# Output stage of a hybrid decoder step: conditioning loads issued by GpSimd, and the order of two small products in the SSD part

## The chip, the cores and the metric

One core of one Trainium2 chip. The metric is the device time of one execution in microseconds (us); several runs give a median. Weights come from HBM in the course of the kernel, so both TensorE and the 16 DMA engines matter.

## The reference

One layer of a decoder works on 288 tokens at once: 256 of a prompt and 8 x 4 of samples, with width 2048, in float32.

```python
mod = silu(c) @ w_ada + b_ada                      # 6 parts: sh1, sc1, g1, sh2, sc2, g2
h = rmsnorm(x, norm1) * (1 + sc1) + sh1
u_pool, z, xbc, dt_raw = split(h @ w_in)
pool_out = pool_mixer(u_pool)                      # trailing means, a linear map per group
ssd_out = ssd_mixer(z, conv(xbc), dt_raw)          # below
x = x + g1 * (concat(pool_out, ssd_out) @ w_out)   # the output stage
h2 = rmsnorm(x, norm2) * (1 + sc2) + sh2
x = x + g2 * conv_ffn(h2)                          # gate and val, conv of gate, w_down
y = rmsnorm(x, norm_f)
```

The SSD mixer has 24 heads of 64 in 4 groups. In a chunk, y = (C B^T * decay) x dt is summed with what the state at the chunk's start gives, then comes D x, a gate and a norm. For the samples that second part is one product with the state handed in, `yo` in the kernel.

## The kernel before, in words

All token matrices lie as channels x tokens: 16 tiles of 128 channels (k) by 288 tokens. A projection takes for each output tile m the weight in two halves of 128 x 1024 float32 (512 KB, `raw_out_3_0` is the first half of output tile 3). A half is loaded by `load` (L279, one DMA), cast by ScalarE to its high part `whi` (L298), and VectorE subtracts to get the low part `wlo` (L300). TensorE then makes three products for each k (`mm3`, L312 to L314): whi with the high operand, whi with the low one, wlo with the high one.

Buffers of `raw` come from rings. In the output stage 8 are used for weights (`raw`), and others for the conditioning (`rawa`); `whi` and `wlo` have 4 each. A load waits until its buffer was read for the last time, and what is queued behind it on the issuing engine waits too.

The conditioning (`mod` of the reference) is computed beside the other work. `ada_visits` (L421) loads pieces of w_ada (512 KB each, `raw_adap_4_6_1`: part 4, k=6, half 1) and multiplies them with silu(c) in `whole` (L414), 32 products of 128 x 512 in a *visit*. In the output stage, part 4 has four visits of 4 k's, so 8 loads each; the visits stand on TensorE behind the output tiles m=3, 6, 9 and 12. All loads are issued by SyncE (SP, L279).

In the SSD part, `ssd_group` runs for four groups g beside the projections, in steps cut by `yield`. The main loop pulls one step between stretches of a projection, so that ScalarE and VectorE make an operand while TensorE does something else. One step made the transposes of B (L794 to L796), the next the product C B^T (L799 to L805) and two DMAs to `sbx`. `outputs` (L864) forms for each t in 0, 1, 2 (two heads) an output in one PSUM tile: the sample columns NP:N sum the product of `yo` (L868) and two of `xdt` with the decays `e` (L872); the other columns are for the prompt.

In the output stage, `out_units(m)` (L1131) makes tile m in two accumulators: `mm_out` for the SSD operands, which VectorE then scales (`oz`, L1179), and `mm_outp` for the pool operands. `residual` (L1168) adds both to x: VectorE makes the prompt's part (L1169) and `rs` (L1172), POOL adds rs to x (L1175). `squares` squares the finished tile on ScalarE (`sqa`, L1185) and POOL adds it to `rt` (L1189). x itself is loaded by SyncE four tiles at a time (L1213). Later parts of the program are allocated and begun when their buffers allow: POOL's load of `stf` (L1280) and two copies into `gb` (L1292) are of the FFN stage, but a scheduler places them in the output stage.

The order of instructions on each engine is decided by a scheduler when the program is built: each engine has one fixed list and works through it in order. A change of which engine issues a load changes the lists of several engines.

Of the kernel before, what the change touches and what calls it, by code (L numbers as in the profile page):

```python
# [18 lines left out]
P = 128  # L19
D = 2048  # L20
KT = D // P
NP = 256
NB, NL = 8, 4
NS = NB * NL
N = NP + NS
# [29 lines left out]
AK, AO = 2, 4  # L55
# [28 lines left out]
def _xbc_chunks(bi):  # L84
    (k0, gk), (a, b) = BLOCKS[bi]
    mper = RAWC // (gk * P)
    cuts = [a, *([4, 8] if bi == 0 else []), *range(a + (12 if bi == 0 else mper), b, mper), b]
    return [(list(range(k0, k0 + gk)), list(range(m, n))) for m, n in zip(cuts, cuts[1:])]
# [35 lines left out]
def _halves(nk):  # L124
    return [(0, 8), (8, nk - 8)]
# [41 lines left out]
def kernel(ctx: ExitStack, tc, ins, outs):  # L167
    nc = tc.nc
    S = _STREAM
    wflat = ins["wflat"]  # L170
# [11 lines left out]
    def aux(name):  # L182
        return px.tile([P, 512], F32, tag="aux", name=name)
# [10 lines left out]
    seli = vec[:, K_SEL:K_SEL + 32]  # L194
# [78 lines left out]

    wp = [None]

    def load(key, ring="raw"):
        off, cols = S.items[key]
        t = wp[0].tile([P, RAWC], F32, tag=ring, name="raw_" + "_".join(map(str, key)))
        nc.sync.dma_start(t[:, :cols], wflat[off:off + P * cols].rearrange("(p n) -> p n", p=P))  # L279
        return t  # L280

    queue = deque(_need_order())
    ahead = {}
    nloads = [0]

    def top_up():

        while queue and nloads[0] - min((n for n, _ in ahead.values()), default=nloads[0]) < RAW0 + RAW1 + RAWA:
            key = queue.popleft()
            ahead[key] = (nloads[0], load(key))  # L290
            nloads[0] += 1
# [4 lines left out]
    def split_steps(raw, a, n, name):  # L296
        hi = wp[0].tile([P, RAWC], F32R, tag="whi", name="whi_" + name)
        yield nc.scalar.copy(hi[:, :n], raw[:, a:a + n])  # L298
        lo = wp[0].tile([P, RAWC], F32R, tag="wlo", name="wlo_" + name)
        yield hi, lo, nc.vector.tensor_tensor(lo[:, :n], raw[:, a:a + n], hi[:, :n].bitcast(F32), ALU.subtract)  # L300
# [37 lines left out]
    def ada_sb(ps, nb, name, r=P):  # L338
        asb = kp.tile([P, 512], F32, tag="asb", name="asb_" + name)
        nc.scalar.copy(asb[0:r, :nb], ps[0:r, :nb])  # L340
        return asb
# [66 lines left out]
    def whole(ps, chunks, step, pin, begun=0):  # L408

        n = 0  # L410
        for k, h, raw in chunks[::-1]:
            for j in (2 * h, 2 * h + 1):
                with tc.high_priority() if n else nullcontext():
                    i = nc.tensor.matmul(ps[32 * j:32 * j + 32, :], sc_c[:, k, :],  # L414
                                         raw[:, 512 * (j % 2):512 * (j % 2) + 512], start=not begun and k == step - 1,
                                         stop=k == KT - step, tile_position=(0, 32 * j))
                if n or pin:
                    tc.keep_in_program_order(i)
                n += 1

    def ada_visits(parts, step, ps=None, begun=0, apart=False):  # L421

        plan = [(part, k0) for part in parts for k0 in range(begun, KT, step)]
        ahead, end = [], None

        def chunks(v):
            part, k0 = plan[v]
            for k in range(k0, k0 + step):
                for h in range(2):
                    ahead.append((k, h, load(("adap", part, k, h), "rawa")))  # L430
                    if apart:
                        yield
            for _ in range(1 if apart else 3):
                yield

        yield from chunks(0)
        for v, (part, k0) in enumerate(plan):
            if end:
                ada_end(*end)
                end = None  # L440
            if k0 == 0:
                ps = pa.tile([P, 512], F32, tag="ada", name=f"adap{part}")
            whole(ps, ahead, step, True, begun)
            ahead.clear()
            if k0 + step == KT:
                end = part, ada_sb(ps, 512, f"p{part}")
            yield
            if v + 1 < len(plan):
                yield from chunks(v + 1)
        ada_end(*end)  # L450
        yield

    def ada_end(part, asb):
        pt = ada_tr(asb, 512, f"p{part}")
        with tc.high_priority():
            nc.vector.tensor_tensor(ada[:, part].rearrange("p (j i) c -> p i j c", j=4),
                                    pt.rearrange("p (i j c) -> p i j c", i=4, j=4)[:, :, :, 0:NC9],
                                    bada[:, part].rearrange("p (j i) -> p i j", j=4).unsqueeze(3)
                                    .to_broadcast([P, 4, 4, NC9]), ALU.add)
        if part == 4:  # L460
            ada_scale(1, 4, vec[:, V_N2:V_N2 + KT], 0, KT)
# [76 lines left out]
    for q in range(4):  # L538
        t = mx.tile([P, 4, N], F32, tag="blk", name=f"xa{q}", bufs=4)
# [232 lines left out]
    def ssd_group(g):  # L772
# [10 lines left out]
        xdt = kp.tile([P, 3, G6], F32, tag="hmod", name=f"xdt{g}", bufs=2)  # L783
# [10 lines left out]
        for c in range(3):  # L794
            nc.tensor.transpose(pt[:, c * P:(c + 1) * P], toks(3, c), ident)
        nc.scalar.copy(bt.rearrange("p c n -> p (c n)"), pt[:, 0:3 * P])  # L796

        yield
        pcb = aux(f"cb{g}")  # L799
        for c in range(3):  # L800
            n = min(P, N - c * P)
# [5 lines left out]
        q = slice(NS * g, NS * g + NS)  # L807
        nc.gpsimd.dma_start(sbx[q, 0:P], bt[0:NS, 2, :])
        nc.gpsimd.dma_start(sbx[q, P:P + G6], xde[0:NS, 2, :])
        yield  # L810

        s1 = sx[0].tile([P, G6], F32, tag="s1", name=f"s1_{g}")
# [24 lines left out]
        yo = sx[0].tile([P, G6], F32, tag="yo", name=f"yo{g}")  # L837
# [26 lines left out]
        def outputs(t, e, ec):  # L864
            assert (g, t) in zdone
            pq = aux(f"y{g}_{t}")
            rows = [slice(0, 64), slice(64, P)]
            nc.tensor.matmul(pq[:, NP:N], yo[:, P * t:P * t + P], seli, start=True, stop=False)  # L868
            for i, r in enumerate(rows):
                f = slice(64 * (2 * t + i), 64 * (2 * t + i) + 64)  # L870
                f = slice(64 * (2 * t + i), 64 * (2 * t + i) + 64)
                nc.tensor.matmul(pq[r, NP:N], xdt[:, 2, f], e[:, i, NP:N], start=False, stop=True)  # L872
            for i, r in enumerate(rows):
                f = slice(64 * (2 * t + i), 64 * (2 * t + i) + 64)
                nc.tensor.matmul(pq[r, 0:P], xdt[:, 0, f], e[:, i, 0:P], start=True, stop=True)
            for i, r in enumerate(rows):
                f = slice(64 * (2 * t + i), 64 * (2 * t + i) + 64)
                nc.tensor.matmul(pq[r, P:NP], xdt[:, 1, f], e[:, i, P:NP], start=True, stop=False)
                nc.tensor.matmul(pq[r, P:NP], s1[:, f], ec[:, i, :], start=False, stop=True)
            yt = cf[:, t, 0:N]  # L880
            nc.vector.scalar_tensor_tensor(out=yt, in0=yt,
                                           scalar=vec[:, V_D + 3 * g + t:V_D + 3 * g + t + 1],
                                           in1=pq[:, :N], op0=ALU.mult, op1=ALU.add)
            zt = zy[g][:, t, :]
            nc.vector.tensor_tensor(zt, zt, yt, ALU.mult)
            sq = kp.tile([P, N], F32, tag="xsq", name=f"ysq{g}_{t}", bufs=2)
            nc.scalar.activation(sq, zt, AF.Square)
            if g + t == 0:
                nc.gpsimd.tensor_copy(ssq, sq)
            else:  # L890
                nc.gpsimd.tensor_tensor(ssq, ssq, sq, ALU.add)
# [9 lines left out]
        outputs(1, *dec[1])  # L901
        yield
        outputs(2, *dec[2])
        yield

# [54 lines left out]
    adas = ada_visits((2, 3), AK)  # L960
    with in_order(*(e.engine for e in (nc.tensor, nc.scalar, nc.vector))):
# [3 lines left out]
        for q in range(4):  # L965
# [5 lines left out]
            for i in range(4):  # L971
                nc.tensor.matmul(ssum[32 * i:32 * i + 32, :N], ones[:, 0:32], sq[:, i, :],
                                 start=(q == 0), stop=(q == 3), tile_position=(0, 32 * i))
# [16 lines left out]
        parts = [split_steps(t, 0, len(ms) * P, f"xbc0_{i}") for i, (t, (_, ms)) in  # L990
                 enumerate(zip(first, _xbc_chunks(0)))]
# [36 lines left out]
    def take(gn, n):  # L1028
        for _ in range(n):
            next(gn)  # L1030
            yield

    ssd3 = ssd_group(3)
    back = chain(conv0, h0s(0), zip2(ssd_group(0), conv_group(1)), h0s(1),
                 zip2(ssd_group(1), conv_group(2)), h0s(2), zip2(ssd_group(2), conv_group(3)), h0s(3),
                 zip2(take(ssd3, TK), chain(pool_units(UEARLY[0]), pool_units(UEARLY[1]))))
    credit = {}
# [9 lines left out]
    for bi in range(len(BLOCKS)):  # L1047
        last = bi + 1 == len(BLOCKS)
        top_up()
        if last:  # L1050
# [6 lines left out]
            raw = load(("dt",))[:, :KT * NH].rearrange("p (k h) -> p k h", h=NH)  # L1057
# [6 lines left out]
            ps = pm.tile([P, 512], F32, tag="mm", name="mm_dt")  # L1064
# [26 lines left out]
    n = 0  # L1091
# [13 lines left out]
            next(late[m])  # L1105
    drain(adas)
    wp[0].move("rawa", "rawa", "raw")
    adas = ada_visits((4,), AO, apart=True)
    for h, (_, n) in enumerate(_halves(KT)):
        ready[("out", 0, h)] = split(load(("out", 0, h)), 0, n * P, f"out_0_{h}")  # L1110
    drain(back)
# [11 lines left out]
    for g in range(4):  # L1123
        for t in range(3):
            k = 4 + 3 * g + t
# [273 lines left out]
    with in_order(nc.sync.engine, nc.scalar.engine, nc.vector.engine):  # L1399
        for i, (m0, n, own) in enumerate(YC):  # L1400
            v = x[:, m0:m0 + n, :]
            eng, r = (nc.gpsimd, rstdf) if own else (nc.vector, rstdp)
# [148 lines left out]
```

## Time and profile before

| | us |
|---|---|
| median of 3 runs | 1345.59 (1345.21 to 1346.12) |
| profiled execution | 1346.4 |
| its span | 1344.6 |
| TensorE busy in the span | 1328.4 |
| VectorE, ScalarE, GpSimd busy | 822.8, 580.3, 223.1 |
| SSD groups in the span (about) | 250 to 362 |
| output stage in the span | 361.4 to 488 |

The profile is a trace of one execution. Its page gives each engine's busy time, the DMA queues, the waits and the costliest groups of instructions; other views show a timeline of one engine, the busy time in chosen windows, or one tile. In a row, `PE` is TensorE, `PEld` its weight loads, `DVE` VectorE, `ACT` ScalarE, `POOL` GpSimd, and `SP` or `SPq` SyncE and its queue of DMA issues. `out<-in` names the tiles. Brackets at a row's end give the idle time of the engine ahead of the instruction and what released it. There are two queues for the DMAs of the program: q1 (hardware_dynamic) carries 310.72 MB that SyncE and ScalarE issue, q0 (software_dynamic) 9.69 MB that POOL issues.

### The profile page before, as it was taken

To read this page: it belongs to the slowest core of one execution; us is meant where nothing else is said; L and a number is where in the kernel's file an instruction comes from. 1 tells how busy PE (TensorE), PEld (TensorE's weight loads), DVE (VectorE), ACT (ScalarE), POOL (GpSimd) and SP (SyncE) were. 2 spreads that over 40 slices of the span, in tenths; PEclk is the share of its full clock that TensorE was granted. 3 is DMA by queue.
4 is the path that set the end of the run, shared out by engine and by line. 5 is a ranking of instruction groups with operands and counts; after the bars stand their busy time and mean duration, and the time that the engine had idled before them with its cause. 6 is when DMAs were issued, how large, how long until landed. Compare 5 with 4: busy or idle time off the path is not lost.

```text
span 1344.6 us, 26157 instructions
## 1 busy us (share of the span) xinstructions
PE 1328.4 (99%) x10523; PEld 1247.1 (93%) x10523; DVE 822.8 (61%) x1375; ACT 580.3 (43%) x913; POOL 223.1 (17%) x449
## 2 busy tenths in 40 slices
PE   9999999999999999999999999999999999999997
PEld 7899988776788889999999999999999999999997
DVE  5776569878754568555565455665655556666543
ACT  5243244677733335433433333434433334443552
POOL 0000012123122222102121001221210011122221
PEclk9999999999999999999999999999999999999999
DMA  9999778888898866687455455555544555555521
GB/s 375 405 370 373 272 266 308 308 318 299 306 402 354 324 237 228 229 311 282 172 201 171 167 179 184 203 185 196 182 162 172 190 190 193 194 190 191 188 69 71
DMA packets 97482, 323.19 MB, mean 240 GB/s; under 512 B 10768, under 2 KB 19920, under 8 KB 97360
## 3 DMA queue, kind: packets, MB, share of 16 engines
q1 hardware_dynamic: 93456, 310.72, 63.0%
q0 software_dynamic: 3184, 9.69, 2.0%
q8 instruction: 82, 1.34, 0.4%
q10 hardware_dynamic: 720, 1.11, 0.2%
q14 instruction: 40, 0.33, 0.1%
HBM read 309.78 MB, written 10.39 MB: 238 GB/s over the span
## 4 chain that ended last, share of the span: by engine, by line
PE 93%; DMA 3%; DVE 2%; ACT 1%; issue 0%; POOL 0%; SPq 0%; DVEq 0%; ACTq 0%; POOLq 0%
PE mm_down L313 7%; PE mm_down L312 7%; PE mm_down L314 7%; PE mm_val L313 6%; PE mm_gate L313 6%; PE mm_gate L312 6%; PE mm_gate L314 6%; PE mm_val L314 6%; PE mm_val L312 6%; PE xbc L312 4%; PE xbc L313 4%; PE xbc L314 4%; PE adap L414 4%; PE adag L381 2%; DMA raw_adap<-wflat 2%; PE mm_out L314 2%
## 5 line engine op out<-in xcount | busy, mean ns | idle before, releaser
L313 PE MATMUL mm_down<-al,whi_down 128*128 128x288 f32 x688 | 202.5, 294 | 0.0
L312 PE MATMUL mm_down<-ah,whi_down 128*128 128x288 f32 x688 | 202.4, 294 | 0.0
L314 PE MATMUL mm_down<-ah,wlo_down 128*128 128x288 f32 x688 | 202.0, 294 | 0.0
L313 PE MATMUL mm_val<-h2l,whi_val 128*128 128x288 f32 x640 | 189.1, 296 | 0.0
L313 PE MATMUL mm_gate<-h2l,whi_gate 128*128 128x288 f32 x640 | 189.1, 295 | 0.0
L314 PE MATMUL mm_val<-h2h,wlo_val 128*128 128x288 f32 x640 | 188.4, 294 | 0.0
L314 PE MATMUL mm_gate<-h2h,wlo_gate 128*128 128x288 f32 x640 | 188.4, 294 | 0.0
L312 PE MATMUL mm_gate<-h2h,whi_gate 128*128 128x288 f32 x640 | 188.3, 294 | 0.0
L312 PE MATMUL mm_val<-h2h,whi_val 128*128 128x288 f32 x640 | 188.0, 294 | 0.0
L300 DVE TENSOR_TENSOR wlo_down<-raw_down,whi_down 128x1024 fp32r<-128x1024 f32 x96 | 109.1, 1137 | 115.4 <-ACT whi_down L298 115.4
L300 DVE TENSOR_TENSOR wlo_gate<-raw_gate,whi_gate 128x1024 fp32r<-128x1024 f32 x80 | 98.9, 1237 | 131.5 <-ACT whi_gate L298 131.5
L298 ACT CAST whi_down<-raw_down 128x1024 fp32r<-128x1024 f32 x96 | 92.3, 962 | 164.7 <-PE mm_down L313 135.3
L298 ACT CAST whi_gate<-raw_gate 128x1024 fp32r<-128x1024 f32 x80 | 84.1, 1051 | 156.6 <-PE mm_gate L313 80.3
L298 ACT CAST whi_val<-raw_val 128x1024 fp32r<-128x1024 f32 x80 | 84.1, 1052 | 129.3 <-issue 110.1
L312 PE MATMUL xbc<-h1h,whi_xbc 128*128 128x288 f32 x448 | 133.1, 300 | 0.8 <-ACT h1h L491 0.7
L313 PE MATMUL xbc<-h1l,whi_xbc 128*128 128x288 f32 x448 | 132.3, 296 | 0.0
L314 PE MATMUL xbc<-h1h,wlo_xbc 128*128 128x288 f32 x448 | 130.1, 295 | 0.0
L312 PEld LDWEIGHTS mm_down<-ah,whi_down 128*128 128x128 f32 x688 | 129.2, 188 | 0.0
L313 PEld LDWEIGHTS mm_down<-al,whi_down 128*128 128x128 f32 x688 | 129.1, 188 | 0.0
L314 PEld LDWEIGHTS mm_down<-ah,wlo_down 128*128 128x128 f32 x688 | 129.0, 188 | 0.0
L312 PEld LDWEIGHTS mm_gate<-h2h,whi_gate 128*128 128x128 f32 x640 | 120.3, 188 | 2.5 <-issue 2.5
L314 PEld LDWEIGHTS mm_gate<-h2h,wlo_gate 128*128 128x128 f32 x640 | 120.5, 188 | 0.0
(337 smaller groups left out, 2978.8 us busy)
## 6 DMA issues: line engine op xcount, KB each, us to landing
raw_adap<-wflat SPq DMA_DIRECT2D x128, 512.0 KB, 6.6
raw_gate<-wflat SPq DMA_DIRECT2D x80, 512.0 KB, 3.5
raw_val<-wflat SPq DMA_DIRECT2D x80, 512.0 KB, 3.5
raw_ada<-wflat SPq DMA_DIRECT2D x64, 512.0 KB, 9.6
raw_xbc<-wflat SPq DMA_DIRECT2D x50, 512.0 KB, 9.8
raw_down<-wflat SPq DMA_DIRECT2D x48, 512.0 KB, 3.4
raw_out<-wflat SPq DMA_DIRECT2D x32, 512.0 KB, 9.7
raw_down<-wflat SPq DMA_DIRECT2D x32, 384.0 KB, 3.5
```

Source lines behind the costliest of these rows:

```text
L298: yield nc.scalar.copy(hi[:, :n], raw[:, a:a + n])
L300: yield hi, lo, nc.vector.tensor_tensor(lo[:, :n], raw[:, a:a + n], hi[:, :n].bitcast(F32), ALU.subtract)
L312: nc.tensor.matmul(ps, whi[:, w], bh, start=first, stop=False)
L313: nc.tensor.matmul(ps, whi[:, w], bl, start=False, stop=False)
L314: nc.tensor.matmul(ps, wlo[:, w], bh, start=False, stop=last)
L381: i = nc.tensor.matmul(ps[32 * j:32 * j + 32, :nb], sc_c[:, ck, :], raw[:, c:c + nb], start=q0 + n == 0, stop=q0 + AQ[gi] >= nq and n + 1 ...
L414: i = nc.tensor.matmul(ps[32 * j:32 * j + 32, :], sc_c[:, k, :], raw[:, 512 * (j % 2):512 * (j % 2) + 512], start=not begun and k == step - 1,
```

## The change

`load` and `ada_visits` get a parameter for the issuing engine, and the visits of the output stage (part 4) pass GpSimd. In `outputs`, for t=0 and 1 the products of xdt and e open the accumulation of the sample columns and yo's product closes it; for t=2 it is as before. The step with the transposes of B goes on with C B^T, and the `yield` between them moves behind the two DMAs.

```diff
-    def load(key, ring="raw"):
+    def load(key, ring="raw", eng=nc.sync):
...
-        nc.sync.dma_start(t[:, :cols], wflat[off:off + P * cols].rearrange("(p n) -> p n", p=P))
+        eng.dma_start(t[:, :cols], wflat[off:off + P * cols].rearrange("(p n) -> p n", p=P))
...
-    def ada_visits(parts, step, ps=None, begun=0, apart=False):
+    def ada_visits(parts, step, ps=None, begun=0, apart=False, eng=nc.sync):
...
-                    ahead.append((k, h, load(("adap", part, k, h), "rawa")))
+                    ahead.append((k, h, load(("adap", part, k, h), "rawa", eng)))
...
         nc.scalar.copy(bt.rearrange("p c n -> p (c n)"), pt[:, 0:3 * P])
-
-        yield
         pcb = aux(f"cb{g}")
...
         nc.gpsimd.dma_start(sbx[q, P:P + G6], xde[0:NS, 2, :])
+        yield
         yield
...
-            nc.tensor.matmul(pq[:, NP:N], yo[:, P * t:P * t + P], seli, start=True, stop=False)
+            own = t < 2
+
+            def from_yo(start):
+                nc.tensor.matmul(pq[:, NP:N], yo[:, P * t:P * t + P], seli, start=start, stop=not start)
+
+            if not own:
+                from_yo(True)
             for i, r in enumerate(rows):
                 f = slice(64 * (2 * t + i), 64 * (2 * t + i) + 64)
-                f = slice(64 * (2 * t + i), 64 * (2 * t + i) + 64)
-                nc.tensor.matmul(pq[r, NP:N], xdt[:, 2, f], e[:, i, NP:N], start=False, stop=True)
+                nc.tensor.matmul(pq[r, NP:N], xdt[:, 2, f], e[:, i, NP:N], start=own, stop=not own)
+            if own:
+                from_yo(False)
...
-    adas = ada_visits((4,), AO, apart=True)
+    adas = ada_visits((4,), AO, apart=True, eng=nc.gpsimd)
```

Three places show how the lists of the engines change; the numbers at a name's end are the builder's own. First SyncE at the start of the output stage, before:

```order
L279 DMA raw_out_2_1_4849<-wflat 128x1024
L279 DMA raw_adap_4_0_0_4757<-wflat 128x1024
L279 DMA raw_adap_4_0_1_4777<-wflat 128x1024
L279 DMA raw_adap_4_1_0_4803<-wflat 128x1024
L279 DMA raw_adap_4_1_1_4833<-wflat 128x1024
L1213 DMA x_4715<-x 128x1152 x2
L279 DMA raw_adap_4_2_0_4847<-wflat 128x1024
L279 DMA raw_adap_4_2_1_4879<-wflat 128x1024
L279 DMA raw_out_3_0_4896<-wflat 128x1024
```

And the same place of the change:

```order
L279 DMA raw_out_2_1_4849<-wflat 128x1024
L279 DMA raw_out_5_0_5074<-wflat 128x1024
L279 DMA raw_out_5_1_5108<-wflat 128x1024
L279 DMA raw_out_6_0_5155<-wflat 128x1024
L1219 DMA x_4715<-x 128x1152 x2
L279 DMA raw_out_3_0_4896<-wflat 128x1024
L279 DMA raw_out_3_1_4930<-wflat 128x1024
```

The adap loads are gone from the list, and the loads of out_5_0, out_5_1 and out_6_0 stand where they stood, ahead of out_3_0.

Second ScalarE, at the casts of the output tiles 5 to 7, before (sqa_4 is the square of the finished tile m=4):

```order
L1185 ACTIVATE sqa_4_5068<-x_4715 128x288
L298 CAST whi_out_5_1_5110<-raw_out_5_1_5108 128x1024
L298 CAST whi_out_6_0_5157<-raw_out_6_0_5155 128x1024
L1185 ACTIVATE sqa_5_5150<-x_4715 128x288
L298 CAST whi_out_6_1_5191<-raw_out_6_1_5189 128x1024
L298 CAST whi_out_7_0_5252<-raw_out_7_0_5250 128x1024
```

And of the change:

```order
L298 CAST whi_out_5_1_5110<-raw_out_5_1_5108 128x1024
L1191 ACTIVATE sqa_3_4987<-x_4715 128x288
L298 CAST whi_out_6_0_5157<-raw_out_6_0_5155 128x1024
L298 CAST whi_out_6_1_5191<-raw_out_6_1_5189 128x1024
L298 CAST whi_out_7_0_5252<-raw_out_7_0_5250 128x1024
L1191 ACTIVATE sqa_4_5068<-x_4715 128x288
```

The square of m=4 moves from ahead of the cast of out_5_1 to behind that of out_7_0; likewise the cast of out_9_1 stands ahead of sqa_7, where it stood behind sqa_8.

Third POOL, from the load of stf on, before:

```order
L1280 DMA stf_6557<-st_ffn 128x688
L1291 MEMSET gb0_6560 128x2
L1291 MEMSET gb1_6579 128x2
L1292 COPY gb0_6560<-stf_6557 128x8x2
L1292 COPY gb1_6579<-stf_6557 128x8x2
L1175 TENSOR_TENSOR x_4715<-x_4715,rs2_0_4721 128x32
```

In the change, 13 adap loads (0_0 to 6_0) and the additions of m=0 to the first of m=2 stand ahead of it, and then:

```order
L1286 DMA stf_6557<-st_ffn 128x688
...
L1298 COPY gb0_6560<-stf_6557 128x8x2
L1298 COPY gb1_6579<-stf_6557 128x8x2
L1181 TENSOR_TENSOR x_4715<-x_4715,rs2_3_4951 128x32
L279 DMA raw_adap_4_8_1_5294<-wflat 128x1024
L1181 TENSOR_TENSOR x_4715<-x_4715,rs2_3_4984 128x32
L279 DMA raw_adap_4_9_0_5314<-wflat 128x1024
L1195 TENSOR_TENSOR rt2_4716<-rt2_4716,sqa_3_4987 128x288
L279 DMA raw_adap_4_6_1_5138<-wflat 128x1024
L279 DMA raw_adap_4_7_0_5167<-wflat 128x1024
L279 DMA raw_adap_4_7_1_5181<-wflat 128x1024
```

The load of stf and the copies that wait for it stand later, between adap loads, and the last three loads of the second visit stand behind the sum with sqa_3. In the SSD part the lists change only at the moved products and steps; behind the output stage nothing changes but the place of some loads at its end.

## The prediction

> **What bounds the kernel now.** I read the page's span and busy shares first, then TensorE's waits, then the stretch of the output stage in TensorE's, ScalarE's, VectorE's and SyncE's timelines, and last the table of DMA issues.
>
> ```profile
> span 1344.6 us, 26157 instructions
> PE 1328.4 (99%) x10523; PEld 1247.1 (93%) x10523; DVE 822.8 (61%) x1375; ACT 580.3 (43%) x913; POOL 223.1 (17%) x449
> ```
>
> TensorE is busy for 1328.4 of 1344.6 us, so only its own idle time can be won, and nearly any new wait of TensorE is lost in full. The profiled execution took 1346.4 us, 1.8 us outside the span; it lies 0.8 us above the median of 1345.59 us. I work out differences on the profiled execution and add them to the median, taken as 1345.6. Groups of TensorE's waits (us in total, times, longest) that the change may touch:
>
> ```profile
> PE mm_out L314 <- DVE wlo_out L300: 1.5, 4, 0.5
> PE cse L852 <- DVE yo L838: 0.5, 1, 0.5
> PE y L872 <- DVE e L860: 0.4, 1, 0.4
> ```
>
> The output stage has four waits for a low half of a weight (wlo_out), 1.5 us together. What such a wait really costs is read from TensorE's timeline (start, duration, line, operation, and in brackets the idle time with its releaser), here at the output units m=3 and m=6:
>
> ```profile
> 386.42 0.29 PE L313 MATMUL mm_out<-mixl,whi_out 128*128 128x288 f32 x1
> 387.18 0.40 PE L314 MATMUL mm_out<-mixh,wlo_out 128*128 128x288 f32 x1 [0.46 <-DVE wlo_out L300]
> 387.42 0.29 PE L312 MATMUL mm_out<-mixh,whi_out 128*128 128x288 f32 x1
> ...
> 414.20 0.29 PE L313 MATMUL mm_outp<-mixl,whi_out 128*128 128x288 f32 x1
> 414.95 0.40 PE L314 MATMUL mm_out<-mixh,wlo_out 128*128 128x288 f32 x1 [0.45 <-DVE wlo_out L300]
> 415.19 0.29 PE L312 MATMUL mm_out<-mixh,whi_out 128*128 128x288 f32 x1
> ...
> 415.32 0.30 PE L313 MATMUL mm_out<-mixl,whi_out 128*128 128x288 f32 x1
> ```
>
> Undisturbed products start 0.13 us apart (415.19, 415.32). From 386.42 to 387.42 pass 1.00 us for two starts that need 0.26: 0.74 us lost, the idle 0.46 and 0.28 for the restart. From 414.20 to 415.19 it is 0.99, so 0.73 = 0.45 + 0.28. The four waits thus cost 1.5 + 4 x 0.28 = 2.6 us: 0.7 at m=3 and 1.9 at the three later ones.
>
> Why the two kinds arise is seen on ScalarE and VectorE:
>
> ```profile
> 384.39 1.05 ACT L298 CAST whi_out<-raw_out 128x1024 fp32r<-128x1024 f32 x1 [1.47 <-DMA raw_out<-wflat]
> 385.90 1.22 DVE L300 TENSOR_TENSOR wlo_out<-raw_out,whi_out 128x1024 fp32r<-128x1024 f32 x1
> ...
> 404.82 0.44 ACT L1185 ACTIVATE sqa<-x 128x288 f32<-128x288 f32 x1 [6.46 <-POOL x L1175]
> 405.17 1.98 ACT L298 CAST whi_out<-raw_out 128x1024 fp32r<-128x1024 f32 x2
> ...
> 412.25 0.45 ACT L1185 ACTIVATE sqa<-x 128x288 f32<-128x288 f32 x1 [5.10 <-POOL x L1175]
> ```
>
> At m=3 the cast waits for the transfer of raw_out_3_0, which lands at 384.39. The later ones are a matter of order: ScalarE stands at a square of x for 6.46 us although the weight behind it is there, casts at 405.17, and the low half is late. So transfers bound m=3, the order on ScalarE bounds the later waits.
>
> **The late waits: -1.9 us.** In the order of the changed program the casts of out_5_1, out_6_1 and out_9_1 each stand ahead of the square that they stood behind. Nothing else holds these casts: their four buffers come free as TensorE finishes earlier units. The three waits go. What is late next is nothing on TensorE, since the squares feed only POOL's running sum, read at the stage's end.
>
> **m=3: +3.3 us.** Here the change moves transfers. SyncE's timeline and the issue table (KB each, median us from issue to landing):
>
> ```profile
> 367.49 1.75 SPq L279 DMA_DIRECT2D raw_adap<-wflat  x4
> 369.29 1.11 SPq L1213 DMA_DIRECT2D x<-x  x2
> 370.72 1.06 SPq L279 DMA_DIRECT2D raw_adap<-wflat  x2
> 373.78 0.33 SPq L279 DMA_DIRECT2D raw_out<-wflat  x1
> ```
>
> ```profile
> raw_out<-wflat SPq DMA_DIRECT2D x32, 512.0 KB, 9.7
> raw_adap<-wflat SPq DMA_DIRECT2D x128, 512.0 KB, 6.6
> x<-x SPq DMA_DIRECT2D x4, 576.0 KB, 10.0
> stf<-st_ffn POOLq DMA_DIRECT2D x1, 344.0 KB, 4.8
> ```
>
> And the windows of 5 us (stretch, length, busy PE, PEld, DVE, ACT, POOL, clock, DMA share, GB/s):
>
> ```profile
> 375.00:380.00 5.00, 5.00 (x38) 4.73 (x37) 2.80 (x6) 1.05 (x1) 0.24 (x1) 1.00 1.02 412
> 380.00:385.00 5.00, 5.00 (x40) 5.00 (x39) 1.86 (x8) 1.50 (x3) 1.95 (x5) 1.00 1.02 410
> 415.00:420.00 5.00, 5.00 (x44) 3.34 (x48) 3.79 (x7) 0.77 (x2) 1.35 (x2) 1.00 0.35 142
> ```
>
> The DMA engines are full at 375 to 385 with 0.410 MB per us, so out_3_0 lands later by whatever is put ahead of it. Before, ahead of it went six adap loads (0.524 MB each), two of x (0.590) and stf (0.352): 4.68 MB. After, SyncE puts out_5_0, out_5_1, out_6_0 and the two of x ahead: 2.75 MB, 3.28 with itself. Meanwhile POOL issues eight adap loads, 4.19 MB, on a queue of its own. Nothing in this trace shows two full queues side by side, so I bound the share from both sides. SyncE's queue served first: 2.75 MB ahead, 1.93 less, landing at most 4.7 us earlier (379.7). POOL's first: 6.94 MB, 2.26 more, 5.5 us later (389.9). Even shares: POOL's queue gets as much as SyncE's, 2.75 + 3.28 = 6.03 MB, 1.35 more, 3.3 us later: 387.7. I take even shares, as no row prefers one queue. On the page "DMA: Bandwidth & Descriptors", section "Issuing engines are not separate DMA queues", the Trainium skill says that DMAs of all issuers run on the same 16 engines and interleave, and that several issuers save only the time to issue; by that, too, the transfers gain nothing and the estimate stays with even shares. No run shows it yet.
>
> From landing to the product it took 387.18 - 384.39 = 2.8 us (cast, queue on VectorE, subtraction). After a landing at 387.7 the product of m=3 starts 3.3 us later than before, at 390.5, and as TensorE was already waiting there, all of it is lost: +3.3 (bounds -0.7, when out_3_0 comes so early that the stall goes, and +5.5). The next halves follow with 0.52 MB each: at half share 2.6 us apart, against 8 x 3 x 0.13 = 3.1 us that TensorE takes for a half, so they keep up.
>
> **The adap loads on POOL: 0, bounds 0 and +12.** SyncE gains room, but POOL now runs 32 issues among its work, in order. Its timeline:
>
> ```profile
> 365.78 0.55 POOL L1280 DMA_DIRECT2D stf<-st_ffn  x1
> 370.67 1.75 POOL L1292 COPY gb<-stf 128x16 f32<-128x16 f32 x2 [4.20 <-DMA stf<-st_ffn]
> 393.53 0.25 POOL L1175 TENSOR_TENSOR x<-x,rs 128x32 f32<-128x32 f32 x1 [4.16 <-DVE rs L1172]
> 394.42 1.10 POOL L1175 TENSOR_TENSOR x<-x,rs 128x32 f32<-128x32 f32 x1 [0.64 <-DVE rs L1172]
> 396.07 0.80 POOL L1189 TENSOR_TENSOR rt<-rt,sqa 128x288 f32<-128x288 f32 x1 [0.55 <-ACT sqa L1185]
> ```
>
> An issue takes 0.55 us, 32 make 17.6 us on an engine that is 17% busy; there is room for them. What counts is what stands behind a waiting issue. Behind those of m=0 to m=2 stand stf and then the gb copies, which wait for its landing (4.20 us before), and behind these x of m=3, the sum with sqa_3, and the loads adap_4_6_1, 7_0 and 7_1, which the second visit (behind m=6 on TensorE) needs:
>
> ```profile
> 396.39 0.33 SPq L279 DMA_DIRECT2D raw_adap<-wflat  x1
> ...
> 417.80 0.64 PE L414 MATMUL adap<-raw_adap,sc_c 128*32 128x512 f32 x4
> ```
>
> SyncE issued them from 396.39 on; the visit began at 417.80. After, they follow rt's sum of m=3, which ended at 396.87 and moves by m=3's 3.3 us to 400.2 at least: issues until 401.9, landing with raw_out's 9.7 us at 411.6, some 8 us before the visit (417.80 + 3.3 less what the waits at m=5 and m=6 cost, about 419.6). I take 0. The other bound: 18 adap loads and stf up to 7_1 are 9.8 MB, at half of 0.410 that is 48 us from 367.5 on, 415.5; if POOL stands besides at stf's landing and the copies as long as SyncE stood at its longest, 11.4 us, and the two delays add, the visit waits 7 us; with loads held at the issue a few more, 12.
>
> ```profile
> SPq L279 <- PE adap L414: 80.4, 32, 11.4
> ```
>
> The row 394.42 shows a POOL operation stretched from 0.25 to 1.10 us where VectorE's subtraction of the next weight runs (the row 393.53 is the same operation without one). If an issue is stretched likewise, it costs 0.85 us more, three of them 2.6 us: inside the 8 us of cover, so the sum stays, and it is one way into rival C. The Trainium skill, page "SBUF — State Buffer", section "SBUF: two separate sides", speaks against the change at this point: a DMA that GpSimd issues needs descriptors that GpSimd writes, and it can't write them while VectorE holds the port that both share. By that rule an issue waits out a whole operation of VectorE; the trace shows the stretch only for the addition, not for an issue (0.55 us).
>
> **The SSD parts: 0, bounds -1.0 and +1.0.** The product of yo in front of a group, among other products:
>
> ```profile
> 309.95 0.30 PE L868 MATMUL y<-vec,yo 128*128 128x32 f32 x2
> 310.09 0.38 PE L312 MATMUL mm_uz<-h1h,whi_uz 128*128 128x288 f32 x1
> 310.31 0.29 PE L313 MATMUL mm_uz<-h1l,whi_uz 128*128 128x288 f32 x1
> ```
>
> It takes 310.31 - 309.95 = 0.36 for it and one wide product of 0.13: 0.23 us. Eight of them (t=0 and 1 of four groups) move behind two narrow products of the same run; no row shows one there. Between free and twice its price each changes by at most 0.13, eight by 1.0 either way; I take 0, the row's own price. Of the two waits above, that for yo (0.5 us) is in front of the decays, which the change leaves there; that for e (0.4 us) is in front of a narrow product, and with yo's product no longer ahead of it it may start 0.2 us sooner and wait that much longer, which is inside the bounds too. Transposes of B and C B^T in one step change a neighbour on TensorE, at most one restart: inside the bounds.
>
> **Sum.** -1.9 + 3.3 + 0 + 0 = +1.4 us: 1345.6 + 1.4 = **1347.0**.
>
> **The rivals.** *Gain (B)*: SyncE's queue is not slowed by POOL's. Then out_3_0 lands before 384, all four waits go, -2.6 us, to 1343.0; with the SSD bounds 1342.0 to 1344.0. For it: SyncE no longer stands 80.4 us at adap loads, and the hole of 142 GB/s at 415 to 420 shows that room exists later. Against it: at 375 to 385 the DMA engines were full. *Starved visit (C), slower*: stf lands late, POOL stands at the gb copies, adap_4_6_1 to 7_1 come behind, and TensorE waits at the second visit. It decides once 7_1 lands after 419.6, which is an issue after about 410. Price 7 us on top of the sum: 1354, from 1349 to 1359. For it: POOL works strictly in order, and eight loads are in front of its first addition; against it: the 8 us of cover. *The change doesn't do what it says (D)*: transfers and casts come when they came before, since the same bytes pass the same full DMA engines and the order on ScalarE follows the data; m=3 and the three later waits keep their price: 1345.6.
>
> **How the numbers follow.** Even shares (A) 0.45, its own range 1344.5 to 1349.5 (SyncE's and POOL's share between even and one-sided, SSD within 1); B 0.20; C 0.27; D 0.08. The range from 1342.0 to 1355.0 holds A, B, D and the lower half of C. A measurement of this kernel can tell about 0.2%, 2.7 us: faster is below 1342.9, slower above 1348.3. Faster: half of B and a little of A, 0.14. Slower: all of C and a quarter of A, 0.38. Within: the rest, 0.48.
>
> **What would show it.** Right: in TensorE's waits, mm_out for wlo_out shrinks to one long wait of some 4 us at m=3, and ScalarE's cast there waits for raw_out until about 387.7. No square stands ahead of the casts at m=5, 6 and 9. B shows as no wait at m=3 at all, C as a wait of the second visit's adap product for raw_adap, with POOL's gb copies standing at stf. Wrong would be a price in the SSD part beyond 1 us: then y's products with yo behind them have long starts. The forecast fails if a queue is favoured, or if the transfers of 32 loads by POOL are themselves slower than those by SyncE.

## The result, and the profile after

The changed kernel takes 1352.09 us in the median of 6 runs (1351.7 to 1353.8), the kernel before 1345.8 (1345.21 to 1346.21, 6 runs): ratio 1.0049 with a 95% interval of 1.0036 to 1.0062. It is slower by 6.3 us by the medians, 6.6 by the ratio. The forecast was 1347.0, with a range of 1342.0 to 1355.0: the sign is right, the size (+1.4) more than four times too small. The time lies inside the whole range, but above the range that even shares had for themselves (1344.5 to 1349.5); that part of the whole range was there for rival C. So it is luck that the range holds the time.

The page and TensorE's waits in the output stage after the change (361 to 490 us; us in total, times, longest):

```profile
span 1350.2 us, 26174 instructions
PE 1331.7 (99%) x10523; PEld 1251.1 (93%) x10523; DVE 821.5 (61%) x1375; ACT 581.9 (43%) x913; POOL 239.8 (18%) x481
```

```profile
PE mm_out L312 <- ACT whi_out L298: 4.6, 1, 4.6
PE mm_out L314 <- DVE wlo_out L300: 0.4, 1, 0.4
```

Instead of four waits for a low half there is one long one for a high half, at m=3. It stands where the prediction put its long wait, though that one was for the low half. ScalarE's timeline shows what it hangs on, TensorE's what it costs:

```profile
386.93 0.44 ACT L1191 ACTIVATE sqa<-x 128x288 f32<-128x288 f32 x1 [8.98 <-POOL x L1181]
390.73 1.04 ACT L298 CAST whi_out<-raw_out 128x1024 fp32r<-128x1024 f32 x1 [3.37 <-DMA raw_out<-wflat]
```

```profile
391.83 0.61 PE L312 MATMUL mm_out<-mixh,whi_out 128*128 128x288 f32 x1 [4.63 <-ACT whi_out L298]
392.24 0.44 PE L313 MATMUL mm_out<-mixl,whi_out 128*128 128x288 f32 x1
393.09 0.61 PE L314 MATMUL mm_out<-mixh,wlo_out 128*128 128x288 f32 x1 [0.41 <-DVE wlo_out L300]
393.50 0.45 PE L312 MATMUL mm_out<-mixh,whi_out 128*128 128x288 f32 x1
393.74 0.45 PE L313 MATMUL mm_out<-mixl,whi_out 128*128 128x288 f32 x1
...
398.30 0.37 PE L314 MATMUL mm_out<-mixh,wlo_out 128*128 128x288 f32 x1
398.50 0.29 PE L312 MATMUL mm_out<-mixh,whi_out 128*128 128x288 f32 x1
```

raw_out_3_0 lands at 390.7, where it landed at 384.4 before. And there is a second loss, which the forecast did not have: behind the idle time the products start 0.24 us apart (393.50, 393.74), and not 0.13, until 398.30. The windows have the reason in their eighth number, the granted clock:

```profile
385.00:390.00 5.00, 2.20 (x17) 1.96 (x15) 2.60 (x8) 0.44 (x1) 3.23 (x8) 1.00 1.03 411
390.00:395.00 5.00, 2.76 (x10) 2.41 (x11) 2.75 (x4) 2.44 (x3) 2.54 (x3) 0.66 1.02 409
395.00:400.00 5.00, 5.00 (x28) 5.00 (x28) 2.85 (x5) 2.65 (x3) 0.79 (x2) 0.66 1.03 409
400.00:405.00 5.00, 5.00 (x46) 2.54 (x45) 4.96 (x9) 1.77 (x3) 2.05 (x4) 1.00 1.03 409
```

In windows of 1 us the clock is 0.50 from 392 to 398.

Where the time went is read by comparing the start of the same product in both traces. Three pairs, each the row of before and then that of the change:

```profile
374.38 0.38 PE L312 MATMUL mm_outp<-mixh,whi_out 128*128 128x288 f32 x1
...
390.19 0.29 PE L312 MATMUL mm_out<-mixh,whi_out 128*128 128x288 f32 x1
...
467.81 0.40 PE L312 MATMUL mm_out<-mixh,whi_out 128*128 128x288 f32 x1
```

```profile
375.12 0.38 PE L312 MATMUL mm_outp<-mixh,whi_out 128*128 128x288 f32 x1
...
398.50 0.29 PE L312 MATMUL mm_out<-mixh,whi_out 128*128 128x288 f32 x1
...
473.97 0.40 PE L312 MATMUL mm_out<-mixh,whi_out 128*128 128x288 f32 x1
```

| stretch | lag at its end, us | in this stretch | forecast |
|---|---|---|---|
| up to the output stage (SSD) | 0.74 | +0.74 | 0 (-1.0 to +1.0) |
| m=3, first half | 8.31 | +7.57 | +3.3 (-0.7 to +5.5) |
| the rest of the output stage | 6.16 | -2.15 | -1.9, visits 0 |
| up to the last w_down product | 6.23 | +0.07 | 0 |

The first row can't be told from the difference between two executions. At the first of the three products the traces of two later versions whose SSD part is that of before stand 0.92 us ahead of before (POOL from k=6) and 1.04 us behind it (x later). The +7.57 at m=3 is far beyond that.

The span grew by 5.6 us only, since the last transfers of the output end 0.6 us sooner behind the last product. The 7.57 us at m=3 are 4.80 for the wait (391.83 came 4.93 behind the start before it, where 0.13 is usual), 0.54 for the restart and the second wait (1.28, less the 0.74 that m=3 had cost before), and 20 starts that were 0.11 us longer, 2.23.

### The profile page after: what moved, and what is told of

It reads as the page before. It is cut to its first block, busy times and chain, and to the rows that moved or that the text cites. A ratio compares the mean times of both kernels' runs of the same rounds, so it can differ in the third digit from the quotient of the medians.

```text
span 1350.2 us, 26174 instructions
## 1 busy us (share of the span) xinstructions
PE 1331.7 (99%) x10523; PEld 1251.1 (93%) x10523; DVE 821.5 (61%) x1375; ACT 581.9 (43%) x913; POOL 239.8 (18%) x481
## 4 chain that ended last, share of the span: by engine, by line
PE 93%; DMA 4%; DVE 2%; ACT 0%; issue 0%; POOL 0%; SPq 0%; DVEq 0%; ACTq 0%
PE mm_down L313 7%; PE mm_down L312 7%; PE mm_down L314 7%; PE mm_val L313 6%; PE mm_gate L313 6%; PE mm_gate L312 6%; PE mm_gate L314 6%; PE mm_val L314 6%; PE mm_val L312 6%; PE xbc L312 4%; PE xbc L313 4%; PE xbc L314 4%; PE adap L414 4%; PE adag L381 2%; DMA raw_adap<-wflat 2%; PE mm_out L312 2%
```

## The experiments

The theory after the result: the loss is made by transfers. POOL's loads have a queue of their own, which shares the full DMA engines with SyncE's, so raw_out_3_0 comes late; the idle time then lowers the clock. Rivals: POOL as an issuer is slow or blocks; the loads of out_5 and out_6 ahead of out_3_0 are the cause alone; the SSD part makes it.

**One part at a time.** The kernel before with the loads issued by POOL, and nothing else:

```diff
-    adas = ada_visits((4,), AO, apart=True)
+    adas = ada_visits((4,), AO, apart=True, eng=nc.gpsimd)
```

> The kernel before with the first part alone: the 32 adap loads of part 4 issued by POOL, the SSD part as before. The trace of the change puts TensorE 0.74 us behind before at the start of m=3 and 6.23 us behind from the end of the output stage on. Theory (transfers): all but the SSD's 0.74 belongs to this part, so 5.5 us over before, about 1351.3, with one TensorE wait of about 4.6 us at m=3, raw_out_3_0 landing at about 390 and the granted clock falling after it. Rival (the parts act together, the SSD's delay makes the wait long): 3 us over before or less, and a wait of at most 4 us at m=3.

Measured: 1351.89 against 1346.61, ratio 1.0037 (1.0025 to 1.005), so 5.0 us. TensorE's waits:

```profile
PE mm_out L312 <- ACT whi_out L298: 4.0, 1, 4.0
PE adap L414 <- DMA raw_adap<-wflat: 0.5, 1, 0.5
```

The cast that it waits for begins at 388.89, released by raw_out, about 1 us before the 390 of the theory, and the wait is as long as the rival allowed (4 us); the time decides for the theory. The second row is the second visit, which waits for a load of POOL here. The part by itself has most of the loss; the SSD part isn't needed for it.

yo's product last for t=0 and 1, and nothing else:

```diff
-            nc.tensor.matmul(pq[:, NP:N], yo[:, P * t:P * t + P], seli, start=True, stop=False)
+            own = t < 2
...
+            if own:
+                from_yo(False)
```

> The kernel before with the second part alone: yo's product closes the run for t=0 and 1. Theory: it costs about 0.8 us (eight moved products, 0.1 us each), so about 1346.6, and the merged step gives 0.1 back. Rival: it costs nothing (1345.8) and the merged step makes the 0.74 us.

Measured: 1348.74 against 1346.61, ratio 1.0015 (1.0006 to 1.0024), 2.0 us. The theory had 0.8, the lower end of the interval; the rival is out. What one group costs is seen in the two traces. Before, one group with t=0 or 1, its yo elsewhere:

```profile
262.54 0.31 PE L872 MATMUL y<-e,xdt 128*64 128x32 f32 x4
262.68 0.42 PE L875 MATMUL y<-e,xdt 128*64 128x128 f32 x4
...
263.14 0.44 PE L879 MATMUL y<-ec,s 128*64 128x128 f32 x4
263.51 0.40 PE L313 MATMUL mm_uz<-h1l,whi_uz 128*128 128x288 f32 x1
```

And with yo's product last (the row of L871; the second one, at 263.49, is the opening product of t=2):

```profile
262.06 0.31 PE L877 MATMUL y<-e,xdt 128*64 128x32 f32 x4
262.29 0.41 PE L871 MATMUL y<-vec,yo 128*128 128x32 f32 x2
262.63 0.44 PE L882 MATMUL y<-e,xdt 128*64 128x128 f32 x4
...
263.12 0.44 PE L886 MATMUL y<-ec,s 128*64 128x128 f32 x4
263.49 0.41 PE L871 MATMUL y<-vec,yo 128*128 128x32 f32 x2
```

From the narrow products to the next kind of work it takes 0.97 us before and 1.43 with yo's product inside, 0.46 more; alone it cost 0.23. Both steps to and from it are longer: 0.23 and 0.34 us where one step of 0.14 was. Eight times 0.46 - 0.23 is 1.8 us, inside the interval. In the trace of this run the lag is 0.57 us at the output stage and 0.99 behind it, less than the median shows; two executions differ by as much.

Transposes of B and C B^T in one step, and nothing else:

```diff
-        yield
         pcb = aux(f"cb{g}")
...
+        yield
         yield
```

> The kernel before with the third part alone: transposes of B and C B^T in one step. Theory: -0.1 us, about 1345.7. Rival: it makes the 0.74 us of the SSD part, about 1346.5.

Measured: 1346.14 against 1346.61, ratio 0.9998 (0.999 to 1.0007): no difference that can be told, as the theory had it. The three parts by themselves give, by their ratios, 5.0 + 2.0 - 0.3 = 6.7 us, the change 6.6.

**POOL issues, but nothing ahead of out_3_0.** The kernel before, where POOL issues from k=6 of part 4 on:

```diff
-                    ahead.append((k, h, load(("adap", part, k, h), "rawa")))
+                    ahead.append((k, h, load(("adap", part, k, h), "rawa", eng if v > 1 or v and k > 5 else nc.sync)))
```

> The kernel before with part 4's loads issued by POOL only from k=6 on (20 of 32), the first 12 by SyncE as before. None of POOL's loads can then go ahead of raw_out_3_0, and the casts of out_5_1, 6_1 and 9_1 stand ahead of the squares as in the change. Theory (transfers ahead of out_3_0 make the loss): the wait at m=3 stays 0.4 to 0.5 us, the three later waits are gone, 2.1 us under before, about 1343.7. Rival (issuing from POOL is itself the loss, by slow or late loads): the visits at m=6, 9 or 12 wait for raw_adap, and the time is at or over before.

Measured: 1343.95 against 1346.61, ratio 0.998 (0.9971 to 0.9989), 2.7 us faster. TensorE's waits in the output stage:

```profile
PE mm_out L314 <- DVE wlo_out L300: 0.5, 1, 0.5
```

One wait is left, that of m=3 as before; the three later ones are gone, and no product of a visit waits. So POOL as an issuer costs nothing that can be told here, with 20 loads of 32 coming from it. As the loss in itself, that rival is out.

**Doses.** POOL issues from k=4 on (`eng if v else nc.sync` in the same line): SyncE's list ahead of out_3_0 is as before, and three of POOL's loads run beside it.

> The kernel before with POOL issuing part 4's loads from k=4 on; SyncE's list ahead of raw_out_3_0 is as before (4.33 MB), but three loads of POOL (4_4_0, 4_4_1, 4_5_0, 1.57 MB) start beside it. Theory (even shares): 1.57 MB more ahead less the 0.35 MB of stf, so out_3_0 lands about 3.0 us later than before, at 387 to 388, TensorE idles 3 to 4 us at m=3, the later waits are gone: some 1347 to 1348, and over that if the granted clock falls at this length of idle too. Rival (only a SyncE list with out_5_0 to 6_0 ahead delays out_3_0): m=3 as before, about 1343.9 as with k=6.

Measured: 1351.44 against 1346.25 (1348.8 to 1356.58, 5 runs), ratio 1.0045 (1.0027 to 1.0062). TensorE's row at m=3:

```profile
390.25 0.61 PE L312 MATMUL mm_out<-mixh,whi_out 128*128 128x288 f32 x1 [4.42 <-ACT whi_out L298]
```

The rival (only out_5 and out_6 ahead of it are to blame) falls: none of them is ahead here, and out_3_0 lands at 389.15. But the theory's size was too small too, 387 to 388 and 1347 to 1348. In its trace the DMA engines moved 291 GB/s at 365 to 370 and 336 at 370 to 375, less than the full 410, and later there is another wait of 1.0 us for a high half, where the forecast had none. The granted clock fell too (0.50 from 389 to 395). What part of the 3 to 4 us over the forecast each of these made wasn't separated.

POOL issues from k=2 on (`eng if v or k > 1 else nc.sync`):

> The kernel before with POOL issuing from k=2 on: SyncE has four adap loads and two of x ahead of raw_out_3_0 (3.28 MB), POOL starts six loads (3.15 MB) beside it. Theory (even shares): 6.43 MB ahead, 1.75 more than before, 4.3 us later, landing at about 388.5 to 389, TensorE idle of 4 to 4.5 us with a lower granted clock after it: 1349 to 1352, near the change although no load of out_5 or out_6 goes ahead. Rival (those loads make the loss): well under 1347.

Measured: 1349.18 against 1346.25, ratio 1.0022 (1.0012 to 1.0031). out_3_0 lands at 388.6, as expected. TensorE's rows at m=3:

```profile
389.71 0.40 PE L312 MATMUL mm_out<-mixh,whi_out 128*128 128x288 f32 x1 [2.80 <-ACT whi_out L298]
389.95 0.29 PE L313 MATMUL mm_out<-mixl,whi_out 128*128 128x288 f32 x1
390.97 0.41 PE L314 MATMUL mm_out<-mixh,wlo_out 128*128 128x288 f32 x1 [0.73 <-DVE wlo_out L300]
391.22 0.29 PE L312 MATMUL mm_out<-mixh,whi_out 128*128 128x288 f32 x1
391.35 0.30 PE L313 MATMUL mm_out<-mixl,whi_out 128*128 128x288 f32 x1
...
391.88 0.44 PE L314 MATMUL mm_out<-mixh,wlo_out 128*128 128x288 f32 x1
392.12 0.44 PE L312 MATMUL mm_out<-mixh,whi_out 128*128 128x288 f32 x1
```

The time is at the lower end of the forecast, the wait shorter than forecast (2.8 and 0.7, not 4 to 4.5). The products run at full clock first and drop to starts of 0.24 us from 391.88 on, 5.0 us after TensorE fell idle at 386.9.

The loss doesn't grow with the number of POOL's loads beside out_3_0: three of them (k=4) gave 1351.4, with runs far apart, and six (k=2) 1349.2. That such loads beside it make the loss is shown by both against k=6; how long it gets is not explained by their bytes alone.

**Can m=3 be had too?** POOL from k=6 on, and x loaded later, which takes one load of x from ahead of out_3_0:

```diff
-XM = (0, 2, 5, 9)
+XM = (0, 4, 7, 10)
```

> POOL issues from k=6 on, and x is loaded by SyncE at m = 0, 4, 7, 10 and not at 0, 2, 5, 9, which takes 0.59 MB from ahead of raw_out_3_0. Theory: out_3_0 lands 1.4 us earlier and the 0.7 us of m=3 go besides: 0.7 us under the version from k=6, so about 3 us under before, 1343.2. Rival (m=3 then waits for something else, or the residual for x): no difference from the version from k=6.

Measured: 1342.93 against 1346.25, ratio 0.998 (0.9972 to 0.9989), 3.3 us faster by the medians; by the intervals that can't be told from the version from k=6. In the trace, a run of 1343.8, no output product waits for a weight any more; in the stage only this is left:

```profile
PE adap L414 <- DMA raw_adap<-wflat: 0.4, 1, 0.4
```

The same edit of XM on the kernel before, with SyncE issuing all:

> The kernel before with x loaded at m = 0, 4, 7, 10 alone. Theory: the wait at m=3 (0.7 us) goes, the three later ones stay: 0.7 us under before. Rival: nothing, since other waits take its place.

Measured: 1347.62 against 1346.25, ratio 1.0011 (1.0002 to 1.0019), slower by 1.4 us. The theory fell here; the waits in its output stage are

```profile
PE mm_out L314 <- DVE wlo_out L300: 2.9, 8, 0.5
PE mm_out L312 <- ACT whi_out L298: 0.2, 1, 0.2
```

Eight waits for a low half stand where four stood. This trace is of the slowest of the eleven runs (1350.23), so its waits need not be those of the median. The edit moved squares and casts on ScalarE again; in this kernel a row moved in SyncE's list changes the order on the engines that follow.

## Why the prediction was right or wrong, step by step

**The late waits (-1.9): right.** They are gone, and -2.15 us were won behind m=3, after 0.2 us lost at the second visit (below). The run from k=6 shows the gain by itself.

**m=3 (+3.3): right in its mechanism, too small.** Even shares were the right choice. The DMA queues of the changed kernel (packets, MB, share of 16 engines) from 380 to 385 us:

```profile
q1 hardware_dynamic: 272, 1.08, 53.6%
q0 software_dynamic: 272, 0.98, 49.0%
```

Two full queues have half each here, and again from 390 to 395 (1.03 and 1.02 MB). The Trainium skill, page "DMA: Bandwidth & Descriptors", section "Issuing engines are not separate DMA queues", has the DMAs of several issuers interleave on the same 16 engines; the trace agrees, and the half each is read from these rows.

What was too small is the term "POOL's queue gets as much as SyncE's", 3.28 MB until out_3_0 is there. That holds if both queues are full from the start, and they weren't. SyncE's loads of out_5_0, out_5_1 and out_6_0 could only be issued at 368.98, 372.05 and 373.19, when their buffers came free, and the first of x behind them at 373.57; POOL had issued eight loads by then. From 370 to 375 the queues looked like this:

```profile
q0 software_dynamic: 303, 1.13, 63.9%
q1 hardware_dynamic: 143, 0.52, 26.7%
```

And from 360 to out_3_0's landing, 360 to 390.6:

```profile
q1 hardware_dynamic: 1811, 6.73, 57.4%
q0 software_dynamic: 1260, 4.60, 39.2%
```

Of POOL's 4.60 MB, 0.28 are its output o_pool, so 4.32 MB of its adap loads came ahead of or beside out_3_0, 1.04 more than even shares from the start would give. At 0.41 MB per us that is 2.5 of the 3.0 us by which out_3_0 landed after the forecast (390.7, not 387.7). The other 0.5 us aren't taken apart; TensorE itself stood 0.74 us behind there. This splitting is worked out from the trace; no run isolates it.

**The clock: not in the forecast.** 2.23 us of the 7.57, and the slow restart, come from it. A cost of idle time beyond itself was read from waits of 0.5 us (0.28 for the restart) and used for one of 4 us; that doesn't carry over.

**The loads on POOL (0): nearly right in its number, wrong in its reason.** The prediction had the loads of the second visit issued by 401.9 and landed 8 us before the visit. In the changed kernel POOL stood 12.47 us at its first addition, for x, and later at the gb copies for stf, as rival C had it. The last three loads of the visit are the first of the five in the second row:

```profile
407.69 0.33 POOL L1298 COPY gb<-stf 128x16 f32<-128x16 f32 x2 [4.20 <-DMA stf<-st_ffn]
410.39 2.70 POOL L279 DMA_DIRECT2D raw_adap<-wflat  x5
```

That is past the 410 from which rival C was to decide. The visit's first weight load had to wait for a load of raw_adap:

```profile
424.78 0.16 PEld L414 LDWEIGHTS adap<-raw_adap,sc_c 128*32 128x32 f32 x8 [0.37 <-DMA raw_adap<-wflat]
```

The visit's first product started at 424.79, 0.43 us behind the one ahead of it, where it was 0.23 before: 0.2 us lost. The loads were issued 10.2 us later than forecast (from 410.39 on, not 400.2) and took longer to land (12.3 us in the median of those issued from 408 to 414, not 9.7); the visit was only 5.2 us later than forecast (419.6). The 8 us of cover were used up, and that the price stayed at 0.2 us is luck. With the first part alone the same visit waited 0.5 us.

The stretch of issues beside VectorE, for which the prediction named the skill, isn't there. The seven issues from 369.17 on took 3.87 us, 0.55 each, beside two subtractions of VectorE:

```profile
369.17 3.87 POOL L279 DMA_DIRECT2D raw_adap<-wflat  x7 [0.16 <-DMA raw_out<-wflat]
370.81 2.35 DVE L300 TENSOR_TENSOR wlo_out<-raw_out,whi_out 128x1024 fp32r<-128x1024 f32 x2
```

The prediction read the page too widely. The Trainium skill, page "SBUF — State Buffer", section "SBUF: two separate sides", keeps GpSimd from writing descriptors while VectorE runs an operation in a 2-port mode; for an operation with two inputs in SBUF, as this subtraction is, it names a block only on GpSimd operations that read SBUF. The trace agrees: the addition, which reads x and rs, was stretched from 0.25 to 1.10 us, the issue was not.

**The SSD parts (0, -1.0 to +1.0): inside the bounds in the change's trace, beyond them in the single run.** There the part cost 2.0 us (0.8 to 3.2 by the interval), and the sign that the prediction named for that is there, long starts around yo's product. The step "between free and twice its price each changes by at most 0.13" was wrong in itself, since twice a price of 0.23 is 0.23 more; and the moved product costs just twice (0.46).

**Rival B** (all four waits go) didn't come with this change, but with the loads from k=6 on and x later: what it left out was that POOL's early loads go beside out_3_0.

## What to carry to other kernels

A load that is moved to another engine's queue leaves the old queue's order, and with it its place behind what is needed first: where the DMA engines were full, it took half of them here. Keep in one queue, or hold back, the loads that are needed late, and move only those that can't start before the urgent ones have landed. And count a wait of TensorE of some microseconds with the slow clock behind it.

## What the runs showed of the hardware

Idle time of TensorE has a price behind it. With waits of 0.5 us the granted clock stayed at 1.00. After 4.0 us (issue by POOL alone), 4.4 (from k=4) and 4.6 (the change) it was 0.50 when work began again, and after 2.8 and 0.7 us with two starts in between (from k=2) it fell 5.0 us after the idle time began. In windows of 1 us it was back at 1.00 from 397, 396, 399 and 396 on: some 3.5 to 6.5 us of work at half speed, 2.2 us lost in the change. The Trainium skill, page "TensorE: Matmul & The Clock Gate", section "Part 1: The HAM clock gate", puts the fall behind an idle window of some 3.4 us and the return behind a busy one of about the same length; the waits of 4.0 us and more agree with the fall, while the case from k=2 shows one where no single idle time was that long. The slow stretches here are as long as one to two of its windows.

A narrow product (128x32) that fills 128 output rows costs 0.46 us where it stands between products that fill 64, twice what it costs among the wide ones (0.23). All eight of them in the run with yo's product last have the two long steps, of about 0.23 and 0.34 us, around it.
